# Computing the modulation vectors in four 32-column tiles of the tensor engine, and splitting every weight on VectorE

## The chip, the cores and the metric

One core of a Trainium2 chip runs the whole program. The metric is the device time of one execution in microseconds. The kernel before took 2518.86 us, the median of three executions (2513.32 to 2525.78).

## The reference, cut to what matters

Two stacks of layers run one after the other on one sequence of S = 256 tokens of width D = 1024. The first stack mixes with forgetting attention and with latent attention, each followed by a mixture of 16 experts; every norm in it is modulated by vectors made from a single condition vector `c`. The second stack has four mixers (retention, MoBA, differential attention, retention), each followed by an MLP.

```python
c_act = jax.nn.silu(c)                                     # (1, 1024)
for layer in range(2):
    sh1, sc1, g1, sh2, sc2, g2 = jnp.split(c_act @ w_mod[layer] + b_mod[layer], 6, axis=-1)   # w_mod[layer]: 1024 x 6144
    h = modulate(rmsnorm(x, norm_g), sh1, sc1)             # h * (1 + sc1) + sh1
    x = x + g1[:, None, :] * mixer(h)                      # forgetting attention, then latent attention
    h = modulate(rmsnorm(x, ffn_norm_g[layer]), sh2, sc2)
    x = x + g2[:, None, :] * grouped_moe(h)
    # behind layer 0: two more vectors, c_act @ kv_w_mod + kv_b_mod (1024 x 2048), for the keys and values of layer 1
```

So there are 14 modulation vectors of 1024 elements, each the product of the condition vector with a 1024 x 1024 piece of a matrix: 4 MB of float32 weights are read for every one of them, and used once.

## The kernel before, in words

**Phases.** The first block runs `start`, `fgt` (forgetting attention), `moe0`, `lat_pre` and `lat_heads` (latent attention) and `moe1`; the second block `ret0`, `mlp0`, `moba`, `mlp1`, `diff`, `mlp2`, `ret1` and `mlp3`. By TensorE's first product of each phase these are, in us of the span: 0 to 44, 44 to 232, 232 to 532, 532 to 579, 579 to 704, 704 to 997; then 997 to 1221, 1221 to 1409, 1409 to 1574, 1574 to 1760, 1760 to 1936, 1936 to 2122, 2122 to 2329 and 2329 to 2522.

**Weights.** A piece of weights of 1 MB is loaded by SyncE's queue into one of five buffers `raw` (`load()`). For the dense layers `unit()` then makes two halves of it in pieces of 128x1024: ScalarE casts `wh` (L147), and `wl = raw - wh` (L153) is what the cast left out. Each dense product is three products of these halves (`wh` by the activation's high half, `wh` by its low half, `wl` by its high half; L169 to L171, L180 to L182, L197 to L199). Which engine makes `wl` is set by the table `SPL`: in five phases every `wl` (in `lat_heads` every second one) goes to GpSimd, in all others to VectorE:

```python
SPL = {'fgt': (1, 0), 'latpre': (1, 0), 'latheads': (2, 0), 'moba': (1, 0), 'diff': (1, 0)}
sh = SPL.get(self.ph, ())
eng = nc.gpsimd if sh and self.nu % sh[0] in sh[1:] else nc.vector
```

127 of the 526 splits are GpSimd's. The experts' weights in the two MoE phases aren't split: there float32 products read `raw` and pairs of other buffers, and two experts' streams of 64 columns stand side by side in the array (L1347).

**Modulations.** `prepare()` puts silu(c) into a tile `c` of 128x8 (element k * 128 + p in row p, column k). `mod()` makes one vector in four steps, of which each loads 4 rows of 128 by 512 columns. On VectorE a step multiplies every row piece by its element of `c` and adds it to an accumulator `macc` of 128x512 (L811 for the first of eight, L813 for the rest). After two steps, half of the vector is there in 128 partial sums per column, and `total()` sums them with four small float32 products (`macc` as the stationary operand, a column of ones moving, L824) into four columns of the result.

The 56 steps stand in a list, `self.queue`. `fill()` takes all or some of them, and `spare()`, called between the pieces of the mixers, takes as many as the next entry of a table (`PLAN0`, `PLAN1`) says. A step's four operations are issued in one go, and the `total()` of the vector before behind the first of them. 8 steps run in the start, 24 in forgetting attention, 4 in the first MoE, 5 in `lat_pre` and 15 in `lat_heads`. In the start, the eight steps of the first two vectors are put in another order, so that the first halves of both come first (L1506).

**Order of the work.** A tile scheduler orders each engine's instructions from the order in the program and the buffers (`pat()`, `ppj()` and `psc()` hand out banks of PSUM: for `pat()` two in most phases and six in `lat_pre`). Each engine works its own list off in order.

**The chains spoken of below.** In `moba` and `diff` the scores need normed queries and keys: L648 sums squares of 8 heads, L652 scales them, the inverse root is worked out by tiny integer and float operations on VectorE (L253 to L263, over 128x16 there and 128x1 or 128x2 elsewhere), L657 and L659 multiply, and TensorE transposes the result (L663). The softmax takes maxima as it moves the scores out of PSUM (L531) and turns them into the bias of the exponential (L533, 128x2). In `diff` the output of a head is normed once more (the same root, L259 among it) into `o` (L710), which TensorE transposes (L210). In `lat_pre`, L869 makes the low half `h2l` of an activation that the projections read.

Of the kernel before, what the change touches and what calls it, by code (L numbers as in the profile page):

```python
# [10 lines left out]
F32 = mybir.dt.float32  # L11
# [4 lines left out]
OP = mybir.AluOpType  # L16
# [14 lines left out]
GU = 2  # L31
GE = 4
HOLD = dict(ret0=2, mlp0=2, mlp1=2, mlp2=2, mlp3=2, moba=4)
SPL = {'fgt': (1, 0), 'latpre': (1, 0), 'latheads': (2, 0), 'moba': (1, 0), 'diff': (1, 0)}
HL = 6
WX = 2
HOMES = "rhrhxhrhrhxhr"
# [47 lines left out]
class Net:  # L85
# [51 lines left out]
    def unit(self, ap, k, n):  # L137
# [4 lines left out]
        for k0 in range(0, k, step):  # L142
# [5 lines left out]
            self.nu += 1  # L148
            sh = SPL.get(self.ph, ())
            eng = nc.gpsimd if sh and self.nu % sh[0] in sh[1:] else nc.vector  # L150
# [568 lines left out]
    def prepare(self):  # L719
# [31 lines left out]
        self.ones = self.b1.tile([128, 128], F32, name="ones", tag="ones")  # L751
        nc.vector.memset(self.ones, 1.0)

    def rope(self):

        nc, I = self.nc, self.I
        pi = self.b1.tile([128, NT], I32, name="pi", tag="pi")
        nc.scalar.dma_start(pi, I["positions"].rearrange("b (t p) -> p (b t)", p=128))
        pf = self.b1.tile([128, NT], F32, name="pf", tag="pf")
        nc.vector.tensor_copy(pf, pi)  # L760
        inv = self.b1.tile([128, 16], F32, name="inv", tag="inv")
        nc.scalar.dma_start(inv, bass.AP(tensor=self.C["narrow"].tensor, offset=self.C["narrow"].offset + 768,
                                         ap=[[0, 128], [1, 16]]))
        ang = self.b1.tile([128, NT, 16], F32, name="ang", tag="ang")
        n = self.b1.tile([128, NT, 16], F32, name="angn", tag="angn")
        for t in range(NT):
            nc.vector.tensor_scalar(ang[:, t, :], inv, pf[:, t:t + 1], None, op0=OP.mult)
        big = 12582912.0
        nc.vector.tensor_scalar(n, ang, 1.0 / (2 * math.pi), big, op0=OP.mult, op1=OP.add)
        nc.vector.tensor_scalar(n, n, big, None, op0=OP.subtract)  # L770
        c1 = 6.28125
        c2 = float((np.array([2 * math.pi - c1], np.float32).view(np.uint32) & np.uint32(0xfffff000)).view(np.float32)[0])
        c3 = 2 * math.pi - c1 - c2
        for cc in (c1, c2, c3):
            nc.vector.scalar_tensor_tensor(ang, n, -cc, ang, op0=OP.mult, op1=OP.add)
        s = self.b1.tile([128, NT, 16], F32, name="hs", tag="hs")
        nc.scalar.activation(s, ang, AF.Sin, scale=0.5)
        nc.vector.scalar_tensor_tensor(ang, ang, -1.0, ang, op0=OP.mult, op1=OP.max)
        nc.vector.tensor_scalar(ang, ang, -0.5, math.pi / 2, op0=OP.mult, op1=OP.add)
        nc.scalar.activation(n, ang, AF.Sin)  # L780
        self.rc = self.b1.tile([128, NT, 2, 16], F32, name="rc", tag="rc")
        self.rsn = self.b1.tile([128, NT, 2, 16], F32, name="rsn", tag="rsn")
        for j in range(2):
            nc.vector.scalar_tensor_tensor(self.rsn[:, :, j, :], s, 2.0, n, op0=OP.mult, op1=OP.mult)
            nc.vector.scalar_tensor_tensor(self.rc[:, :, j, :], s, -2.0, s, op0=OP.mult, op1=OP.mult)
        nc.vector.tensor_scalar(self.rc, self.rc, 1.0, None, op0=OP.add)
# [5 lines left out]

    def mod(self, w, c0, bias, gain=None):
        nc = self.nc
        self.nmod += 1
        col = self.b1.tile([128, 8], F32, name="mod", tag="mod%d" % self.nmod)

        spot = {}  # L800

        def step(u):
            half = u // 2
            r = self.load(self.rows(w, u % 2 * 4, 4, c0 + half * 512, 512), 4, 512)
            if u % 2 == 0:
                spot["acc"] = self.mods.tile([128, 512], F32, name="macc", tag="macc")
            acc = spot["acc"]
            for k in range(4):
                kk = u % 2 * 4 + k
                if kk == 0:  # L810
                    i = nc.vector.tensor_scalar(acc, r[:, k, :], self.c[:, 0:1], None, op0=OP.mult)  # L811
                else:
                    i = nc.vector.scalar_tensor_tensor(acc, r[:, k, :], self.c[:, kk:kk + 1], acc, op0=OP.mult,  # L813
                                                       op1=OP.add)
            with self.tc.issue_after(i.ins):
                self.finish()
            if u % 2:
                self.finish = lambda: total(acc, slice(4 * half, 4 * half + 4))

        def total(acc, c):  # L820
            self.finish = lambda: None
            ps = self.pat()
            for f in range(4):
                nc.tensor.matmul(ps[:, f:f + 1], acc[:, f * 128:f * 128 + 128], self.ones[:, 0:1], start=True, stop=True)  # L824
            self.mark = nc.vector.tensor_tensor(col[:, c], ps[:, 0:4], bias[:, c], OP.add).ins
            if gain is not None:
                nc.vector.scalar_tensor_tensor(col[:, c], col[:, c], 1.0, gain[:, c], op0=OP.add, op1=OP.mult)
        self.queue += [lambda u=u: step(u) for u in range(4)]
        return col

# [655 lines left out]
    def first_block(self):  # L1486
        I = self.I
        with self.tc.tile_pool(name="b1", bufs=1) as b1, \
                self.tc.tile_pool(name="mods", bufs=2) as mods:
            self.b1, self.mods = b1, mods  # L1490
            self.queue, self.plan = [], []
            self.finish = lambda: None
            self.nmod = 0
            self.plan = list(PLAN0)

            def layer(i, j, gain=None):

                return self.mod(I["w_mod"][i], j * D, self.column("b_mod", (6 * i + j) * D), gain)

            with self.phase("start"):  # L1500
                self.prepare()
                self.norm_x()
                ffn = [self.column("ffn_norm_g", i * D) for i in range(2)]
                SH = layer(0, 0)
                A = layer(0, 1, self.column("a_norm_g", 0))
                self.queue = [self.queue[i] for i in (0, 1, 4, 5, 2, 3, 6, 7)]  # L1506
                self.fill()
                self.make_bias()
                self.finish()

            def rope():
                with self.tc.issue_after(self.mark):
                    self.rope()

            def router(i):
                self.finish()
                spot.append(self.router(i, A1, SH1))

            G = layer(0, 2)
            SH1 = layer(0, 3)  # L1520
            A1 = layer(0, 4, gain=ffn[0])
            self.queue.append(lambda: router(0))
            spot = []
            self.queue.append(rope)
            G1 = layer(0, 5)
            kSH = self.mod(I["kv_w_mod"], 0, self.column("kv_b_mod", 0))
            kA = self.mod(I["kv_w_mod"], D, self.column("kv_b_mod", D), self.column("kv_norm_g", 0))
            SH2 = layer(1, 0)
            A2 = layer(1, 1, gain=self.column("b_norm_g", 0))
            self.forgetting(A, SH, G)  # L1530
            self.moe(0, A1, SH1, G1, spot[0])
            SH, A = SH2, A2
            self.left = len(self.queue)
            G = layer(1, 2)
            SH1 = layer(1, 3)
            A1 = layer(1, 4, gain=ffn[1])
            self.queue.append(lambda: router(1))
            G1 = layer(1, 5)
            self.plan = list(PLAN1)
            self.latent(kA, kSH, A, SH, G)  # L1540
            self.moe(1, A1, SH1, G1, spot[1])
            self.pending = self.diag
# [47 lines left out]
```

## Time and profile before

| | |
|---|---|
| median of three executions | 2518.86 us |
| the profiled execution | 2524.33 us, of which its span 2522.5 us |
| mean granted clock of TensorE | 0.955 of 2.4 GHz |
| PE busy | 2276.9 us (90%), 13606 instructions |
| VectorE (DVE) busy | 1310.5 us (52%), 2465 instructions |
| ScalarE (ACT) busy | 985.5 us (39%), 1622 instructions |
| GpSimd (POOL) busy | 297.4 us (12%), 139 instructions |
| DMA | 541.96 MB, 215 GB/s over the span |

The busy shares are averages over phases with different limits, so they are read by phase. "PE" is TensorE's products and "PEld" its loads of stationary weights, which overlap with them; DVE, ACT, POOL and SP are VectorE, ScalarE, GpSimd and SyncE. The granted clock is the mean of two levels, 1.2 GHz (0.5) and 2.4 GHz (1.0), in the stretch. L153 is line 153 of the kernel before; the changed kernel's lines stand 5 to 7 further down from `prepare()` on.

### The profile page before, as it was taken

Reading aid. Unit: us, or ns where it says so; the run is one execution under the profiler, and the core shown is the slowest. Engines: PE = TensorE matmul, PEld = TensorE weight load, DVE = VectorE, ACT = ScalarE, POOL = GpSimd, SP = SyncE. Lnnn points to the kernel's source line nnn. Section 1 sums busy time; section 2 is a strip of 40 time slices with the busy share of each in tenths; the row PEclk is TensorE's granted clock in tenths of the full one; section 3 lists DMA queues with packets and bytes.
Section 4 is the critical chain, followed back from the end, with each engine's and each line's share of the span. In section 5 each row is a group of like instructions: output and inputs, shape, how many; then the busy total and the mean of one; then the engine's idle time right before and its main releaser. Section 6 shows DMA issues by size and latency. Waiting matters only on the chain.

```text
span 2522.5 us, 34039 instructions
## 1 busy us (share of the span) xinstructions
PE 2276.9 (90%) x13606; PEld 1779.1 (71%) x13606; DVE 1310.5 (52%) x2465; ACT 985.5 (39%) x1622; POOL 297.4 (12%) x139
## 2 busy tenths in 40 slices
PE   4887999959989997979999888999678999999999
PEld 3787443348854333867899778998677998887997
DVE  7877110087840003645655544655667555665654
ACT  2444111146521112434444445444455444444443
POOL 2443000032200000000000443001441000000000
PEclk9888999979989998989999989999899999999999
DMA  9768999956689995554555423555423555544552
GB/s 302 244 206 290 348 365 395 354 191 206 228 306 400 397 387 212 165 169 150 167 191 191 158 79 117 170 198 169 135 87 125 190 185 182 176 151 155 177 191 84
DMA packets 310470, 541.96 MB, mean 215 GB/s; under 512 B 15752, under 2 KB 158720, under 8 KB 310304
## 3 DMA queue, kind: packets, MB, share of 16 engines
q1 hardware_dynamic: 298288, 528.84, 60.3%
q10 hardware_dynamic: 12016, 10.85, 1.4%
q8 instruction: 111, 1.82, 0.3%
q14 instruction: 55, 0.45, 0.1%
HBM read 538.57 MB, written 4.22 MB: 215 GB/s over the span
## 4 chain that ended last, share of the span: by engine, by line
PE 50%; DVE 7%; ACT 1%; issue 1%; ACTq 1%; DMA 0%
DVE rsa L259 1%; ACTq L588 1%; DVE wl L153 1%; DVE rsy L253 1%; DVE rsy L263 1%; DVE m L533 1%; DVE rsy L254 0%; DVE p L531 0%; PE acc__mlp__16304 L199 0%; PE acc__mlp__19715 L198 0%; PE acc__mlp__9577 L199 0%; PE acc__mlp__16302 L199 0%; PE acc__mlp__9576 L197 0%; PE acc__mlp__9575 L199 0%; PE acc__mlp__19713 L198 0%
## 5 line engine op out<-in xcount | busy, mean ns | idle before, releaser
L147 ACT CAST wh<-raw 128x1024 fp32r<-128x1024 f32 (+4 forms) x526 | 523.8, 1020 | 462.0 <-issue 71.8
L153 DVE TENSOR_TENSOR wl<-raw,wh 128x1024 fp32r<-128x1024 f32 (+1 forms) x399 | 476.4, 1215 | 380.7 <-ACT wh L147 378.0
L153 POOL TENSOR_TENSOR wl<-raw,wh 128x1024 fp32r<-128x1024 f32 (+4 forms) x127 | 287.3, 2280 | 1577.9 <-ACT wh L147 1570.3
L813 DVE SCALAR_TENSOR_TENSOR macc<-raw,c,macc 128x512 f32<-128x512 f32 x196 | 190.6, 973 | 5.6 <-DMA raw<-in_w_mod_dram 2.4
L535 ACT ACTIVATE p<-p,m 128x128 f32<-128x128 f32 (+1 forms) x128 | 57.0, 448 | 36.5 <-DVE m L533 36.3
L398 ACT CAST aTh<-rl 128x512 fp32r<-128x512 f32 x56 | 34.7, 620 | 78.4 <-DVE rl L396 78.4
L399 DVE TENSOR_TENSOR aTl<-rl,aTh 128x512 fp32r<-128x512 f32 x56 | 38.8, 693 | 38.5 <-ACT aTh L398 38.5
L276 ACT ACTIVATE junk<-x 128x512 f32<-128x512 f32 x52 | 32.7, 629 | 64.5 <-DVE x L341 33.3
L259 DVE SCALAR_TENSOR_TENSOR rsa<-rsy,rsh 128x1 f32<-128x1 f32 x186 | 50.4, 302 | 3.1
L396 DVE TENSOR_TENSOR rl<-rl 128x512 f32<-128x512 f32 x56 | 38.3, 685 | 0.0
L218 ACT CAST hTh<-xg 128x512 fp32r<-128x512 f32 (+1 forms) x36 | 21.2, 604 | 27.5 <-DVE xg L215 24.8
L219 DVE TENSOR_TENSOR hTl<-xg,hTh 128x512 fp32r<-128x512 f32 (+1 forms) x36 | 27.3, 777 | 2.4 <-ACT hTh L218 2.2
L533 DVE TENSOR_SCALAR m<-m 128x2 f32<-128x2 f32 x64 | 26.7, 418 | 0.5
L263 DVE SCALAR_TENSOR_TENSOR rsy<-rsa,rsy 128x2 f32<-128x2 f32 (+2 forms) x141 | 24.9, 177 | 3.9
L648 DVE TENSOR_REDUCE qss<-sq 128x8 f32<-128x512 f32 x16 | 10.9, 684 | 29.1 <-ACT sq L647 29.1
L535 ACT ACTIVATION_READ_ACCUMULATOR p<-p,m 128x1 f32 x128 | 24.1, 189 | 0.0
L1384 PE MATMUL acc__moe__2320<-dv,back 64*128 64x512 f32 x32 | 18.0, 641 | 2.7 <-ACT dv L1375 2.7
L1384 PE MATMUL acc__moe__6093<-dv,back 64*128 64x512 f32 x32 | 18.0, 641 | 2.5 <-ACT dv L1375 2.5
L1384 PE MATMUL acc__moe__2321<-dv,back 64*128 64x512 f32 x32 | 18.0, 641 | 0.0
L1384 PE MATMUL acc__moe__6094<-dv,back 64*128 64x512 f32 x32 | 18.0, 641 | 0.0
L824 PE MATMUL at__latpre__4036<-ones,macc 128*128 128x1 f32 x8 | 1.8, 351 | 16.6 <-DVEq L1231 16.6
L1384 PE MATMUL acc__moe__2323<-dv,back 64*128 64x512 f32 x32 | 16.8, 605 | 0.0
(3889 smaller groups left out, 7365.2 us busy)
## 6 DMA issues: line engine op xcount, KB each, us to landing
raw<-in_w_up_dram SPq DMA_DIRECT2D x64, 1024.0 KB, 5.5
raw<-in_w_down_dram SPq DMA_DIRECT2D x64, 1024.0 KB, 5.5
raw<-in_w_mod_dram SPq DMA_DIRECT2D x48, 1024.0 KB, 5.2
raw<-in_ret_w_in_dram SPq DMA_DIRECT2D x48, 1024.0 KB, 5.2
raw<-in_exp_w_gate_dram SPq DMA_DIRECT2D x40, 1024.0 KB, 12.4
raw<-in_exp_w_down_dram SPq DMA_DIRECT2D x34, 1024.0 KB, 13.0
raw<-in_exp_w_up_dram SPq DMA_DIRECT2D x30, 1024.0 KB, 11.3
wh<-in_exp_w_up_dram SPq DMA_DIRECT2D x34, 512.0 KB, 8.7
```

Source lines behind the costliest of these rows:

```text
L147: nc.scalar.copy(h[:, :m * n], p)
L153: eng.tensor_tensor(l[:, :m * n], p, h[:, :m * n].bitcast(F32), OP.subtract)
L259: nc.vector.scalar_tensor_tensor(a[:, c], y[:, c], h[:, c], y[:, c], op0=OP.mult, op1=OP.mult)
L263: nc.vector.scalar_tensor_tensor(y, a, 1.5, y, op0=OP.add, op1=OP.mult)
L276: nc.scalar.activation(junk[:, :w], p, AF.Square, scale=n ** -0.5, accum_out=ss[:, i, j:j + 1])
L396: nc.vector.tensor_tensor(rl, rl, rl, OP.mult)
L398: nc.scalar.copy(h, rl)
L399: nc.vector.tensor_tensor(aT[1][:, 2 * j:2 * j + 2, :].rearrange("p k t -> p (k t)"), rl, h.bitcast(F32), OP.subtract)
L533: nc.vector.tensor_scalar(mx, mx, -1.0, None, op0=OP.mult)
L535: nc.scalar.activation(p[:, m, :], p[:, m, :], AF.Exp, bias=mx[:, m:m + 1], accum_out=rs[:, m, s:s + 1])
L813: i = nc.vector.scalar_tensor_tensor(acc, r[:, k, :], self.c[:, kk:kk + 1], acc, op0=OP.mult, op1=OP.add)
L1384: mm(acc[tok][half], back[c, e % 4, tok * 128:tok * 128 + 128], dv[c, :], start=e == 0, stop=e == 15)
```

## The change

The modulations' long sums move to TensorE. A step loads 2 rows of 128 by all 1024 columns of its vector, still 1 MB, and makes four float32 products of one bank: the stationary operand is one column of `c`, repeated 32 times, the moving operand 512 columns of one row, and the result 32 partitions of the bank, a tile of 32 columns of the array for each of the four. VectorE then copies the bank into `macc` (first step) or adds it (the three others). Behind the fourth step every row of the four groups of 32 holds a sum: groups 0 and 2 of the first 512 columns, 1 and 3 of the last. `total()` now comes once per vector and adds two rows by products with a small table `pick`, that has a one in rows 0 and 64 (first column) and 32 and 96 (second): eight products instead of twice four. The steps of the start run in their plain order.

With `SPL` empty, every `wl` is made on VectorE.

```diff
-SPL = {'fgt': (1, 0), 'latpre': (1, 0), 'latheads': (2, 0), 'moba': (1, 0), 'diff': (1, 0)}
+SPL = {}
...
+        self.pick = self.b1.tile([128, 2], F32, name="pick", tag="pick")
+        nc.vector.memset(self.pick, 0.0)
+        for j in range(4):
+            nc.vector.memset(self.pick[32 * j:32 * j + 1, j % 2:j % 2 + 1], 1.0)
...
         def step(u):
-            half = u // 2
-            r = self.load(self.rows(w, u % 2 * 4, 4, c0 + half * 512, 512), 4, 512)
-            if u % 2 == 0:
+            r = self.load(self.rows(w, 2 * u, 2, c0, 1024), 2, 1024)
+            ps = self.pat()
+            for k in range(2):
+                for half in range(2):
+                    j = 32 * (2 * k + half)
+                    nc.tensor.matmul(ps[j:j + 32, :], self.c[:, 2 * u + k:2 * u + k + 1].to_broadcast([128, 32]),
+                                     r[:, k, half * 512:half * 512 + 512], start=True, stop=True)
+            if u == 0:
                 spot["acc"] = self.mods.tile([128, 512], F32, name="macc", tag="macc")
-            acc = spot["acc"]
-            for k in range(4):
-                kk = u % 2 * 4 + k
-                if kk == 0:
-                    i = nc.vector.tensor_scalar(acc, r[:, k, :], self.c[:, 0:1], None, op0=OP.mult)
-                else:
-                    i = nc.vector.scalar_tensor_tensor(acc, r[:, k, :], self.c[:, kk:kk + 1], acc, op0=OP.mult,
-                                                       op1=OP.add)
+                i = nc.vector.tensor_copy(spot["acc"], ps)
+            else:
+                i = nc.vector.tensor_tensor(spot["acc"], ps, spot["acc"], OP.add)
             with self.tc.issue_after(i.ins):
                 self.finish()
-            if u % 2:
-                self.finish = lambda: total(acc, slice(4 * half, 4 * half + 4))
+            if u == 3:
+                self.finish = lambda: total(spot["acc"])
...
-        def total(acc, c):
+        def total(acc):
...
-            for f in range(4):
-                nc.tensor.matmul(ps[:, f:f + 1], acc[:, f * 128:f * 128 + 128], self.ones[:, 0:1], start=True, stop=True)
-            self.mark = nc.vector.tensor_tensor(col[:, c], ps[:, 0:4], bias[:, c], OP.add).ins
+            for f in range(8):
+                nc.tensor.matmul(ps[:, f:f + 1], acc[:, f % 4 * 128:f % 4 * 128 + 128], self.pick[:, f // 4:f // 4 + 1],
+                                 start=True, stop=True)
+            self.mark = nc.vector.tensor_tensor(col, ps[:, 0:8], bias, OP.add).ins
...
-                self.queue = [self.queue[i] for i in (0, 1, 4, 5, 2, 3, 6, 7)]
                 self.fill()
```

The change moves instructions on two engines at places that the prediction speaks of. The first is VectorE in `moba`, around the sums of squares of the second group of heads (L648) and the first links of the inverse root (to L263). Before:

```order
L648 TENSOR_REDUCE qss<-sq 128x8
L564 TENSOR_TENSOR o<-at__moba__11565,rs 128x256
L219 TENSOR_TENSOR aTl<-at__moba__11575,aTh 128x2x128
L648 TENSOR_REDUCE qss<-sq 128x8
L652 TENSOR_SCALAR qss<-qss 128x16
L253 TENSOR_SCALAR rsy<-qss 128x16
L255 TENSOR_SCALAR rsh<-qss 128x16
L254 TENSOR_SCALAR rsy<-rsy 128x16
L261 TENSOR_TENSOR rsa<-rsy 128x16
L262 TENSOR_TENSOR rsa<-rsa,rsh 128x16
L263 SCALAR_TENSOR_TENSOR rsy<-rsa,rsy 128x16
```

Now:

```order
L153 TENSOR_TENSOR wl<-raw,wh 128x1024
L219 TENSOR_TENSOR aTl<-at__moba__11646,aTh 128x2x128
L153 TENSOR_TENSOR wl<-raw,wh 128x1024 x2
L648 TENSOR_REDUCE qss<-sq 128x8
L652 TENSOR_SCALAR qss<-qss 128x16
L253 TENSOR_SCALAR rsy<-qss 128x16
L255 TENSOR_SCALAR rsh<-qss 128x16
L254 TENSOR_SCALAR rsy<-rsy 128x16
L261 TENSOR_TENSOR rsa<-rsy 128x16
L153 TENSOR_TENSOR wl<-raw,wh 128x1024
L262 TENSOR_TENSOR rsa<-rsa,rsh 128x16
L263 SCALAR_TENSOR_TENSOR rsy<-rsa,rsy 128x16
```

Four splits now stand here, three ahead of the second sum of squares and one between two links of the root; before they were in the list of GpSimd.

The second place is TensorE in `fgt`, from the end of the decay's products to the score products of the second group (`sc` are banks of scores, `pj` of projections, `at` those that `pat()` hands out). Before:

```order
L972 MATMUL at__fgt__925<-ncum,both 128x256 x2
L523 MATMUL sc__fgt__959<-kT,qT 128x128
L523 MATMUL sc__fgt__999<-kT,qT 128x256
L523 MATMUL sc__fgt__1000<-kT,qT 128x256
L824 MATMUL at__fgt__944<-ones,macc 128x1 x4
L523 MATMUL sc__fgt__999<-kT,qT 128x256
L523 MATMUL sc__fgt__1000<-kT,qT 128x256
L180 MATMUL pj__fgt__1062<-hTh,wh 128x256
```

Now:

```order
L979 MATMUL at__fgt__946<-ncum,both 128x256 x2
L979 MATMUL at__fgt__952<-ncum,both 128x256 x2
L523 MATMUL sc__fgt__1024<-kT,qT 128x256
L523 MATMUL sc__fgt__1025<-kT,qT 128x256
L523 MATMUL sc__fgt__1024<-kT,qT 128x256
L814 MATMUL at__fgt__960<-raw,c 32x512 x4
L814 MATMUL at__fgt__968<-raw,c 32x512 x4
L523 MATMUL sc__fgt__1025<-kT,qT 128x256
L814 MATMUL at__fgt__976<-raw,c 32x512 x4
L545 MATMUL at__fgt__1005<-ident,p 128x128
```

Where one total of four small products stood, three steps of four 32-column products (L814) stand between and behind the score products.

## Rows read from the trace of the kernel before

**Rows 1.** The page, costliest groups (busy us, mean ns, idle before, releaser)
```profile
L153 DVE TENSOR_TENSOR wl<-raw,wh 128x1024 fp32r<-128x1024 f32 (+1 forms) x399 | 476.4, 1215 | 380.7 <-ACT wh L147 378.0
...
L813 DVE SCALAR_TENSOR_TENSOR macc<-raw,c,macc 128x512 f32<-128x512 f32 x196 | 190.6, 973 | 5.6 <-DMA raw<-in_w_mod_dram 2.4
...
L824 PE MATMUL at__latpre__4036<-ones,macc 128*128 128x1 f32 x8 | 1.8, 351 | 16.6 <-DVEq L1231 16.6
```

**Rows 2.** Busy time by stage: stretch, its length, busy us (instructions) by engine
```profile
core 0: us, PE busy (x) PEld busy (x) DVE busy (x) ACT busy (x) POOL busy (x), PEclk, DMA share, GB/s
0.00:44.00 44.00, 9.53 (x36) 7.60 (x36) 27.42 (x59) 6.37 (x12) 3.99 (x6) 1.00 0.92 311
44.00:232.00 188.00, 161.34 (x1168) 151.87 (x1168) 152.59 (x280) 82.83 (x172) 80.44 (x33) 0.89 0.70 234
232.00:532.00 300.00, 268.01 (x1327) 110.60 (x1325) 62.69 (x144) 51.49 (x95) 11.94 (x8) 0.94 0.94 352
532.00:579.00 47.00, 36.20 (x212) 32.58 (x213) 43.50 (x81) 26.91 (x54) 17.97 (x8) 0.86 0.61 205
579.00:704.00 125.00, 115.77 (x753) 105.67 (x752) 97.02 (x257) 69.81 (x164) 24.94 (x13) 0.93 0.67 225
1409.00:1574.00 165.00, 136.67 (x1017) 127.92 (x1016) 85.39 (x212) 83.02 (x171) 70.85 (x32) 0.93 0.36 115
1760.00:1936.00 176.00, 131.31 (x947) 123.56 (x946) 120.11 (x369) 84.11 (x201) 71.22 (x32) 0.89 0.34 109
```

**Rows 3.** Busy time of line L813 alone in forgetting attention
```profile
core 0: us, DVE busy (x), PEclk, DMA share, GB/s
44.00:232.00 188.00, 96.94 (x84) 0.89 0.70 234
```

**Rows 4.** Busy time of line L153 alone, on VectorE and on GpSimd
```profile
core 0: us, DVE busy (x) POOL busy (x), PEclk, DMA share, GB/s
1409.00:1574.00 165.00, 2.52 (x2) 70.85 (x32) 0.93 0.36 115
1760.00:1936.00 176.00, 2.44 (x2) 71.22 (x32) 0.89 0.34 109
```

**Rows 5.** Groups of instructions on VectorE in moba, 1409 to 1574 us
```profile
L533 DVE TENSOR_SCALAR m<-m 128x2 f32<-128x2 f32 x16 | 11.1, 691 | 0.3
...
L253 DVE TENSOR_SCALAR rsy<-qss 128x16 int32<-128x16 int32 x4 | 8.1, 2033 | 0.1
...
L652 DVE TENSOR_SCALAR qss<-qss 128x16 f32<-128x16 f32 x4 | 5.0, 1239 | 0.1
```

**Rows 6.** The same view in retention, 997 to 1221 us
```profile
L259 DVE SCALAR_TENSOR_TENSOR rsa<-rsy,rsh 128x1 f32<-128x1 f32 x30 | 6.3, 219 | 0.9
...
L253 DVE TENSOR_SCALAR rsy<-oss 128x1 int32<-128x1 int32 x8 | 1.2, 153 | 0.3
```

**Rows 7.** The same view in diff, 1760 to 1936 us
```profile
L259 DVE SCALAR_TENSOR_TENSOR rsa<-rsy,rsh 128x1 f32<-128x1 f32 x54 | 21.2, 433 | 0.9
...
L533 DVE TENSOR_SCALAR m<-m 128x2 f32<-128x2 f32 x16 | 8.6, 538 | 0.1
```

**Rows 8.** Timeline of VectorE and GpSimd in diff (start us, duration us, instruction)
```profile
1778.93 11.76 POOL L153 TENSOR_TENSOR wl<-raw,wh 128x1024 fp32r<-128x1024 f32 x5 [5.45 <-ACT wh L147]
...
1783.77 2.32 DVE L253 TENSOR_SCALAR rsy<-qss 128x16 int32<-128x16 int32 x1
1786.01 2.42 DVE L255 TENSOR_SCALAR rsh<-qss 128x16 f32<-128x16 f32 x1
1788.35 2.38 DVE L254 TENSOR_SCALAR rsy<-rsy 128x16 int32<-128x16 int32 x1
```

**Rows 9.** TensorE's waits: waiting line <- releaser: us, times, longest us
```profile
PE pj__latpre__4322 L171 <- DVE h2l L869: 10.1, 2, 7.9
...
PE at__diff__15921 L210 <- DVE o L710: 7.0, 1, 7.0
PE at__moba__11419 L663 <- DVE qk L659: 6.9, 1, 6.9
```

**Rows 10.** Timeline of TensorE in the first MoE (start us, duration us, instruction)
```profile
293.81 0.59 PE L1347 MATMUL pj__moe__2476<-wl,xgt 128*64 128x512 f32 x1
293.82 0.59 PE L1347 MATMUL pj__moe__2476<-raw,xgt 128*64 128x512 f32 x1
294.24 0.59 PE L1347 MATMUL pj__moe__2476<-wl,xgt 128*64 128x512 f32 x1
...
294.77 0.66 PE L1360 MATMUL at__moe__2491<-ident,gu 128*128 128x128 f32 x4
```

More of the change, by code (lines that the diff above doesn't have):

```diff
@@ L826, in total @@
             if gain is not None:
-                nc.vector.scalar_tensor_tensor(col[:, c], col[:, c], 1.0, gain[:, c], op0=OP.add, op1=OP.mult)
+                nc.vector.scalar_tensor_tensor(col, col, 1.0, gain, op0=OP.add, op1=OP.mult)
         self.queue += [lambda u=u: step(u) for u in range(4)]
```

## The prediction

> **What bounds the kernel now.** Read first the busy times stage by stage [rows 2]; a stage is a phase of the program, and its bounds are where TensorE's first product of that phase starts. Two kinds of stage matter. In the mixers of the first block (44 to 232 and 579 to 704 us) TensorE is busy 161 of 188 and 116 of 125 us, VectorE 153 and 97, and the granted clock is 0.89 and 0.93, that is 1.2 GHz instead of 2.4 for 22% and 14% of the time. In the two attention layers of the second block (1409 to 1574 and 1760 to 1936 us) TensorE is busy 137 of 165 and 131 of 176 us: there something else makes it wait. The table of waits says what: the transposes wait up to 6.9 us for qk (L659) in moba and up to 7.0 us for o (L710) in diff, both ends of a chain of tiny VectorE operations [rows 9].
>
> Why that chain is slow is read from the operations themselves. In retention, where GpSimd does nothing, L253 takes 153 ns; in moba, where GpSimd splits weights, the same line takes 2033 ns, L652 1239 and L533 691 [rows 5, 6]. The timeline shows the moment: a run of five splits on GpSimd from 1778.93 to 1790.69 us, 2.35 us each, and inside it one L253 of 16 columns that takes 2.32 us [rows 8]. It waits for the GpSimd instruction to end. L255 and L254 behind it do the same.
>
> **The change, part by part.** 56 steps of modulations leave VectorE (8 in the start, 24 in forgetting attention, 4 in the first MoE, 5 in latpre, 15 in latheads). Each was one L811 and seven L813 per two steps and is now four products on TensorE and one copy or add of 512 columns on VectorE. 127 splits leave GpSimd for VectorE.
>
> *One step on TensorE.* No row shows four column tiles. The nearest shows two, of 64 columns: two matmul records start together (293.81 and 293.82) and the next two 0.43 us later [rows 10]. A float32 product is two such records, so two tiles take 0.86 us. Four at once would also take 0.86, in twos 1.71, one after another 3.42. Leaving the 64-column tiles for a whole-array product costs 0.10 more (294.24 to 294.77, 0.53 instead of 0.43), and each step changes twice: about 1.05 us at full clock is an estimate from these rows, with 3.6 as the other end. I take 1.05, because the two-tile row shows that a second tile costs nothing.
>
> *One step on VectorE.* It loses four operations at 0.97 us on average [rows 1] (1.15 in forgetting, 96.94 us for 84 [rows 3], since GpSimd stands in their way too) and gains one of about 0.7. One split there takes 1.22 us [rows 1] against 2.2 on GpSimd (70.85 us for 32 [rows 4]).
>
> *Start, 0.* Its DMA share is 0.92 [rows 2]: eight units of 1 MB have to land whoever uses them. Bounds: -3 (the last four VectorE operations) and +4 (eight small products in the total instead of four; four take 1.8 us [rows 1]).
>
> *Forgetting, +2.* VectorE falls from 153 by about 105 (L813 and L811), and rises by 24 x 0.7 and 33 x 1.2: some 105 are left, so TensorE is the bound. It gets 24 x 1.05 = 25 us. Floor: all of the 27 idle us filled and the slow clock (22% of 188 us at half speed, some 17 us of busy time) gone, 161 + 25 - 17 = 169, which is -19. Ceiling: nothing filled, +25. In order's listing the new products stand between the score products, where TensorE waits anyway, so I take a value a little under the middle.
>
> *First MoE, +1.* Four steps are 4 us on a TensorE that is busy 268 of 300 us; the VectorE work that held up the branch at its end (TensorE waits 16.6 us there [rows 1]) shrinks. Bounds -4 and +4.
>
> *latpre, -5.* TensorE waits 10.1 us for h2l, which stands behind macc on VectorE [rows 9]; that goes, and 5 x 1.05 comes. Bounds -10 and +3.
>
> *latheads, +6.* TensorE is busy 116 of 125 us; 15 steps are 16 us. Floor: the idle 9 and the half-clock loss of some 8 come back, -1. Ceiling +16.
>
> *moba, -15.* Three lines alone lose to GpSimd: L533 16 x (691 - 153), L253 4 x (2033 - 153), L652 4 x (1239 - 153) = 8.6 + 7.5 + 4.3 = 20 us, all on the chain to qk or p; L254 and L255 are of the same kind and in the same chain, so some 25. In their place come 32 x 1.22 = 39 us of splits, but only where they stand in that chain do they delay it: in the changed order about two of a group's eight do (L153 between L261 and L262, and one among the maxima), 8 x 1.22 = 10. Net -15. Bounds: -28, TensorE's whole idle time, and +10.
>
> *diff, -14.* L259 54 x (433 - 219) = 11.6 and L533 16 x (538 - 153) = 6.2 [rows 6, 7], and the run L253, L255, L254 took some 7 us once instead of 0.5 [rows 8]: 25 to 30 on the chain. More of the splits (32 x 1.22 = 39) stand between its links, about a third, 13. Net -14. Bounds -28 and +12.
>
> The stages after 1936 us have no GpSimd splits and no modulations, nor has the second MoE: 0. Where the VectorE stall goes, TensorE is late next in the first block, and the same chain, without locks, in the second.
>
> **Sum:** 0 + 2 + 1 - 5 + 6 - 15 - 14 = -25 us. The profiled execution took 2524.33 us, 5.5 above the median of 2518.86; set against the median, 2494 us.
>
> A rule speaks against the change. The Trainium skill, "SBUF — State Buffer", section "A bandwidth-pool intuition that's wrong (but worth ruling out)", gives TensorE's reading of the moving operand as about 614 GB/s. By it one step, which streams 128 x 512 float32 values through four tiles twice, 2.1 MB, would take 3.4 us. The trace does not agree: two tiles stream 0.52 MB in 0.43 us [rows 10], 1.2 TB/s. But a limit at twice the page's figure would not show in any row here; that is the next rival.
>
> **Rivals.**
> - *Tiles in twos* (0.15). If TensorE cannot stream more than the two 512-column operands that the rows show at a time, a step takes 0.86 us more. In the 48 steps behind the start that is +41, nearly all on a TensorE that is already the bound there: +16, 2535 us, slower. It decides against the change from a step of some 1.6 us. For it: no row shows four. Against: the second tile is free.
> - *One after another* (0.05). Four streams of 0.86 us, 2.57 more per step, 48 times: +123, about 2617 us. Against it stand the two tiles that do overlap.
> - *The splits take the place of the locks* (0.15). If VectorE's in-order queue delays the chains by as much as GpSimd did, moba and diff gain nothing: +4, 2523 us, no change. For it: 39 us of splits come for 20 to 30 of locks, and in diff a split stands between most links. Against: beside TensorE's projections they cost nothing.
> - *The first block gains too* (0.13). With VectorE half empty the gaps close and the clock stays up: forgetting -15, latheads -1 instead of +2 and +6, so -49, 2470 us. Against: TensorE gets 46 us there and has 36 idle.
>
> **How the numbers follow.** The forecast has 0.52. A measurement of this kernel can tell about 0.5%, 12.6 us, from no change. Faster than 2506: the forecast save 0.02, and the fourth rival, 0.63. Slower than 2531: most of the first rival and the second, 0.19. Between: the third and the edges, 0.18. The range from 2455 to 2540 takes in the fourth rival with the floors of moba and diff, and the first rival; it leaves out the second and the worst of the first.
>
> **What would show it.** Right: L814's records four at a time, 0.43 us from one set of four to the next; L253, L652 and L533 near 150 ns everywhere; TensorE busy over 90% in moba, and its waits for qk and o halved; forgetting attention about as long as before with a clock above 0.93. Wrong: records of L814 that start two by two or one by one; PE's waits for qk as long as before behind L153 on VectorE; or a forgetting stage that is 15 us longer or shorter.

## The result, and the profile after

The changed kernel takes 2458.34 us, the median of four executions (2453.07 to 2466.2), against 2521.63 of the kernel before (four executions too): 63 us less, where 25 were forecast. The ratio, taken of the means, is 0.9756 (95% interval 0.9717 to 0.9794). Its profiled execution took 2453.07 us, so between the two profiles lie 71 us. (The one before stands a little above its median, this one a little below.)

Where the time went is seen by stage, each from TensorE's first product of the phase to that of the next, in us (rounded after subtracting):

| stage | before | after | difference | forecast |
|---|---|---|---|---|
| start | 44.0 | 41.4 | -2.6 | 0 |
| forgetting attention | 188.0 | 179.7 | -8.3 | +2 |
| first MoE | 300.5 | 301.7 | +1.2 | +1 |
| lat_pre | 46.8 | 45.9 | -1.0 | -5 |
| lat_heads | 124.4 | 131.5 | +7.1 | +6 |
| moba | 165.1 | 140.9 | -24.2 | -15 |
| diff | 175.7 | 134.0 | -41.6 | -14 |

The other seven stages came out 1.8 us shorter in all. So the five stages of the first block in the table gave 3.6 us, and two stages of the second block, in which there isn't one modulation, gave 66.

The first view is the busy time by stage of the changed kernel (stretch, its length, busy us and instructions of each engine, granted clock, DMA share, GB/s), to be set beside [rows 2]:

```profile
core 0: us, PE busy (x) PEld busy (x) DVE busy (x) ACT busy (x) POOL busy (x), PEclk, DMA share, GB/s
0.00:41.00 41.00, 21.48 (x99) 7.91 (x100) 9.69 (x36) 5.42 (x11) 0.20 (x4) 1.00 0.90 320
41.00:221.00 180.00, 175.80 (x1353) 145.01 (x1352) 94.74 (x234) 84.05 (x173) 0.00 (x0) 0.96 0.71 245
...
569.00:700.00 131.00, 130.25 (x864) 107.19 (x864) 70.70 (x219) 67.14 (x158) 0.00 (x0) 0.95 0.62 215
1404.00:1545.00 141.00, 129.80 (x1018) 119.75 (x1017) 86.98 (x244) 82.34 (x171) 0.00 (x0) 1.00 0.40 128
1731.00:1865.00 134.00, 123.64 (x945) 114.14 (x944) 108.97 (x401) 81.64 (x199) 0.00 (x0) 0.97 0.45 144
```

In forgetting attention and `lat_heads` TensorE is now busy for 176 of 180 and 130 of 131 us: there it is the bound, and next to nothing is left to fill. In `moba` and `diff` its idle time fell from 28 to 11 and from 45 to 10 us, and for the same products it was busy 7 to 8 us less, with a granted clock of 1.00 instead of 0.93 and of 0.97 instead of 0.89.

Of VectorE's 87.0 and 109.0 us in these two stages, the splits alone are (the same view, line L153 alone):

```profile
core 0: us, DVE busy (x), PEclk, DMA share, GB/s
...
1404.00:1545.00 141.00, 37.87 (x34) 1.00 0.40 128
1731.00:1865.00 134.00, 38.48 (x34) 0.97 0.45 144
```

All other instructions of VectorE are the same as before, 210 in `moba` and 367 in `diff`. Added over their own lengths they took 91.5 and 135.7 us before, and take 60.1 and 95.7 now: 31.5 and 40.0 us less. They take the same 60.1 and 95.7 us in the run with the splits alone, below. So this is time for which GpSimd's splits held them up. (The records of neighbouring instructions overlap a little, so these sums are more than VectorE's busy time.) VectorE's groups in `moba`, beside [rows 5], show the small operations at lengths of 160 to 175 ns:

```profile
L533 DVE TENSOR_SCALAR m<-m 128x2 f32<-128x2 f32 x16 | 2.6, 161 | 0.2
...
L253 DVE TENSOR_SCALAR rsy<-qss 128x16 int32<-128x16 int32 x4 | 0.7, 175 | 0.1
L652 DVE TENSOR_SCALAR qss<-qss 128x16 f32<-128x16 f32 x4 | 0.7, 173 | 0.1
```

Two more lines, L219 and L254, lost some 4 us each. Before:

```profile
L219 DVE TENSOR_TENSOR hTl<-xg,hTh 128x512 fp32r<-128x512 f32 x4 | 6.4, 1629 | 0.1
...
L254 DVE TENSOR_SCALAR rsy<-rsy 128x16 int32<-128x16 int32 (+1 forms) x5 | 5.2, 1037 | 0.0
```

Now:

```profile
L219 DVE TENSOR_TENSOR hTl<-xg,hTh 128x512 fp32r<-128x512 f32 x4 | 2.6, 684 | 0.0
...
L254 DVE TENSOR_SCALAR rsy<-rsy 128x16 int32<-128x16 int32 (+1 forms) x5 | 0.9, 174 | 0.0
```

In `diff` L259 takes 215 ns instead of 433 [rows 7]:

```profile
L259 DVE SCALAR_TENSOR_TENSOR rsa<-rsy,rsh 128x1 f32<-128x1 f32 x54 | 9.3, 215 | 0.4
```

The new step on TensorE, first by its tile (count, then min/median/max of one record in ns, and the first and last start), then in the timeline:

```profile
L814 PE MATMUL at__fgt__858<-raw,c x8: 592/604/616, 99.6 to 100.1; 128*32 128x512 f32 x8
```

```profile
99.63 1.06 PE L814 MATMUL at__fgt__858<-raw,c 128*32 128x512 f32 x8
100.62 0.39 PE L169 MATMUL pj__fgt__875<-wh,hTh 128*128 128x256 f32 x1
```

Eight records of 0.6 us each start within 0.5 us. They start in two sets of four, the second 0.45 us behind the first, so four run at a time, and the next product starts 0.99 us behind the first. The estimate was 1.05.

The Trainium skill ("SBUF — State Buffer", "A bandwidth-pool intuition that's wrong (but worth ruling out)") gives 614 GB/s for TensorE's moving operand in bf16; the prediction left the type out. Taken as a limit for these float32 operands, by which a step would take 3.4 us, the figure does not hold here: the four tiles stream 2.1 MB in 0.99 us, 2.1 TB/s.

### The profile page after: what moved, and what is told of

It is laid out like the page before. It is cut to its first block, busy times and chain, and to the rows that moved or that the text cites. A ratio compares the mean times of both kernels' runs of the same rounds, so it can differ in the third digit from the quotient of the medians.

```text
span 2451.3 us, 34695 instructions
## 1 busy us (share of the span) xinstructions
PE 2315.3 (94%) x14054; PEld 1758.8 (72%) x14054; DVE 1180.6 (48%) x2410; ACT 982.1 (40%) x1622; POOL 10.1 (0%) x12
## 4 chain that ended last, share of the span: by engine, by line
PE 51%; DVE 5%; ACT 1%; ACTq 1%; issue 1%; DMA 0%; DVEq 0%
DVE wl L153 2%; ACTq L588 1%; ACT wh L147 1%; DVE rsa L259 0%; DVE rsy L263 0%; PE acc__mlp__19785 L199 0%; PE acc__mlp__16374 L197 0%; PE acc__mlp__12926 L197 0%; PE acc__mlp__9647 L197 0%; PE acc__mlp__19783 L199 0%; PE acc__mlp__9648 L197 0%; PE acc__mlp__16375 L197 0%; PE acc__mlp__12926 L198 0%; PE acc__mlp__12927 L197 0%; PE acc__mlp__19784 L197 0%
## 5 line engine op out<-in xcount | busy, mean ns | idle before, releaser
L153 DVE TENSOR_TENSOR wl<-raw,wh 128x1024 fp32r<-128x1024 f32 (+4 forms) x526 | 614.2, 1187 | 413.6 <-ACT wh L147 408.9
L259 DVE SCALAR_TENSOR_TENSOR rsa<-rsy,rsh 128x1 f32<-128x1 f32 x186 | 34.4, 215 | 2.7
L219 DVE TENSOR_TENSOR hTl<-xg,hTh 128x512 fp32r<-128x512 f32 (+1 forms) x36 | 23.5, 671 | 2.0 <-ACT hTh L218 1.8
L263 DVE SCALAR_TENSOR_TENSOR rsy<-rsa,rsy 128x2 f32<-128x2 f32 (+2 forms) x141 | 22.6, 160 | 3.4
L535 ACT ACTIVATION_READ_ACCUMULATOR p<-p,m 128x1 f32 x128 | 24.2, 189 | 0.0
L1391 PE MATMUL acc__moe__2359<-dv,back 64*128 64x512 f32 x32 | 18.1, 645 | 4.4 <-ACT dv L1382 4.4
L1391 PE MATMUL acc__moe__6164<-dv,back 64*128 64x512 f32 x32 | 18.0, 641 | 2.7 <-ACT dv L1382 2.7
L1391 PE MATMUL acc__moe__6165<-dv,back 64*128 64x512 f32 x32 | 18.0, 641 | 0.0
L1391 PE MATMUL acc__moe__2360<-dv,back 64*128 64x512 f32 x32 | 18.0, 641 | 0.0
L1391 PE MATMUL acc__moe__2361<-dv,back 64*128 64x512 f32 x32 | 17.2, 618 | 0.0
L1391 PE MATMUL acc__moe__2362<-dv,back 64*128 64x512 f32 x32 | 16.8, 605 | 0.0
L1391 PE MATMUL acc__moe__6166<-dv,back 64*128 64x512 f32 x32 | 16.8, 605 | 0.0
L1391 PE MATMUL acc__moe__6167<-dv,back 64*128 64x512 f32 x32 | 16.8, 605 | 0.0
```

The costliest lines, as they stand in the source:

```text
L153: eng.tensor_tensor(l[:, :m * n], p, h[:, :m * n].bitcast(F32), OP.subtract)
L219: nc.vector.tensor_tensor(lo[:, k0:k0 + n, tok * 128:tok * 128 + 128], pv, d.bitcast(F32), OP.subtract)
L259: nc.vector.scalar_tensor_tensor(a[:, c], y[:, c], h[:, c], y[:, c], op0=OP.mult, op1=OP.mult)
L263: nc.vector.scalar_tensor_tensor(y, a, 1.5, y, op0=OP.add, op1=OP.mult)
L535: nc.scalar.activation(p[:, m, :], p[:, m, :], AF.Exp, bias=mx[:, m:m + 1], accum_out=rs[:, m, s:s + 1])
L1391: mm(acc[tok][half], back[c, e % 4, tok * 128:tok * 128 + 128], dv[c, :], start=e == 0, stop=e == 15)
```

## Experiments

The change has two halves that touch different places. Two theories stood against each other: that the gain is the end of GpSimd's blocking of VectorE, and that it comes from the modulations (or from low halves that are ready earlier). All ratios are to the kernel before, whose median in these runs was 2520.6 to 2520.8 us.

**1. The modulations alone** (`mods_only`): the changed kernel with the old table of splits.

```diff
-SPL = {}
+SPL = {'fgt': (1, 0), 'latpre': (1, 0), 'latheads': (2, 0), 'moba': (1, 0), 'diff': (1, 0)}
```

> The change without its other half: modulations on TensorE, the 127 splits back on GpSimd. Theory of the blocked VectorE (GpSimd's splits hold up VectorE's small operations, and that is nearly all of the gain in the second block): moba is 165 us again instead of 141 and diff 176 instead of 134, so about 2458 + 66 = 2524 us, with the first block within 10 us of that of the changed kernel. Rival, the gain hangs on the modulations (less VectorE work, buffers free earlier): moba and diff stay within 10 us of 141 and 134, and the time under 2480.

Measured: 2548.19 us, 1.0107 (1.0076 to 1.0138): slower than before. `moba` took 166.6 and `diff` 171.7 us, as the first theory says. The first block took 27 us more than in the changed kernel instead of at most 10 (forgetting attention 192.2, `lat_pre` 54.4, `lat_heads` 135.4 us), so GpSimd's splits cost time there too, even with L813 gone. The busy times of forgetting attention and `moba` in this run:

```profile
core 0: us, PE busy (x) PEld busy (x) DVE busy (x) ACT busy (x) POOL busy (x), PEclk, DMA share, GB/s
42.00:234.00 192.00, 181.53 (x1352) 150.93 (x1353) 70.15 (x199) 83.56 (x173) 73.90 (x33) 0.93 0.66 228
...
1431.00:1597.00 166.00, 138.72 (x1015) 130.04 (x1014) 84.81 (x212) 82.77 (x171) 70.57 (x32) 0.92 0.36 115
```

**2. The splits alone** (`splits_only`): the kernel before with the empty table.

```diff
-SPL = {'fgt': (1, 0), 'latpre': (1, 0), 'latheads': (2, 0), 'moba': (1, 0), 'diff': (1, 0)}
+SPL = {}
```

> The other half alone: modulations on VectorE as before, every split on VectorE. Theory of the blocked VectorE: moba 141 and diff 134 us, so some 2522 - 66 = 2456 us; in forgetting attention L813 falls from 1154 ns to some 750, which frees 34 us of VectorE, and 40 us of splits come, so that stage stays within 8 us of its 188. Rival, the modulations on TensorE are needed to make room for the splits in the first block: forgetting attention takes over 196 us and the time is 2465 or more.

Measured: 2422.06 us, 0.9607 (0.958 to 0.9634), and so 36 us faster than the whole change. `moba` 140.7 and `diff` 134.2 us, as expected. Forgetting attention came out at 160.3 us, not within 8 of 188, and `lat_heads` at 116.4:

```profile
core 0: us, PE busy (x) PEld busy (x) DVE busy (x) ACT busy (x) POOL busy (x), PEclk, DMA share, GB/s
44.00:204.00 160.00, 149.30 (x1167) 141.67 (x1168) 137.07 (x312) 82.79 (x172) 0.00 (x0) 0.96 0.82 276
...
545.00:662.00 117.00, 112.15 (x752) 103.47 (x751) 95.12 (x271) 69.06 (x164) 0.00 (x0) 0.96 0.68 232
```

```profile
core 0: us, DVE busy (x), PEclk, DMA share, GB/s
44.00:204.00 160.00, 61.59 (x84) 0.96 0.82 276
```

The second fence is L813 alone: 733 ns each, against 1154 before [rows 3], with the modulations still on VectorE. VectorE does carry both jobs, 137 of 160 us.

The two runs and the two kernels make a square, in us: neither half 2520.6 (2521.6 in the changed kernel's own comparison), modulations alone 2548.2, splits alone 2422.1, both 2458.3. The splits are worth -98.6 by themselves and -89.9 beside the modulations, and the modulations cost +27.6 beside GpSimd's splits and +36.3 without them. By stage, from splits alone to both, the modulations' price is -2.3 in the start, +19.4 in forgetting attention (24 steps), +3.6 in the first MoE (4), +2.6 in `lat_pre` (5) and +15.1 in `lat_heads` (15). In forgetting attention the steps take 26.4 us of TensorE (L814, shown with the next run). TensorE's busy time there grew by just that, from 149.3 to 175.8 us, and only 6.5 us of it came out of its idle time, which fell from 10.7 to 4.2.

**3. Two column tiles instead of four** (`twos`): the price of a step's time on TensorE, changed kernel otherwise.

```diff
-                    j = 32 * (2 * k + half)
+                    j = 32 * half
...
-                                     r[:, k, half * 512:half * 512 + 512], start=True, stop=True)
+                                     r[:, k, half * 512:half * 512 + 512], start=k == 0, stop=k == 1)
```

VectorE's copies and adds and the total take 64 rows accordingly.

> The changed kernel with each step's four products in two column tiles of 32 instead of four, two products one after the other in each, everything else alike. If four tiles really run side by side, a step takes 0.86 us longer: 39 of the 48 steps behind the start lie in forgetting attention and the latent heads, where TensorE is busy 98 and 99% of the time, so +34 to +41 us, 2492 to 2499 us. If four tiles run two by two anyway, 2458 us, no change.

Measured: 2493.27 us, 0.9893 (0.9867 to 0.992), 34.9 more than the changed kernel. L814 alone in forgetting attention, in the changed kernel and then in this one:

```profile
core 0: us, PE busy (x) PEld busy (x), PEclk, DMA share, GB/s
41.00:221.00 180.00, 26.40 (x192) 4.42 (x192) 0.96 0.71 245
```

```profile
core 0: us, PE busy (x) PEld busy (x), PEclk, DMA share, GB/s
40.00:239.00 199.00, 50.01 (x192) 10.22 (x192) 0.96 0.67 229
```

24 steps go from 1.10 to 2.08 us each, 23.6 in all, and the stage grows by 18.7, from 179.7 to 198.4; in `lat_heads` L814 goes from 14.9 to 27.7 us, 12.8 more, and the stage grows by 17.4, from 131.5 to 149.0. Together the two stages grow by 36.1 us for 36.4 more of L814, though neither stage does so by itself; in `lat_heads` the granted clock was also lower, 0.93 instead of 0.95. Four tiles do run side by side, and on a TensorE with few gaps most of what a step takes is paid for. That is how the modulations come to cost 36 us in the square.

**4. The blocking without late halves** (`spare_splits`): every `wl` on VectorE, and the old 127 subtractions once more on GpSimd into a tile that nobody reads.

```diff
+IDLE = {'fgt': (1, 0), 'latpre': (1, 0), 'latheads': (2, 0), 'moba': (1, 0), 'diff': (1, 0)}
...
+            sh = IDLE.get(self.ph, ())
+            if sh and self.nu % sh[0] in sh[1:]:
+                spare = self.sp.tile([128, self.part], F32R, name="spare", tag="spare")
+                nc.gpsimd.tensor_tensor(spare[:, :m * n], p, h[:, :m * n].bitcast(F32), OP.subtract)
```

> The changed kernel, with VectorE making every wl, and beside it the same 127 subtractions once more on GpSimd into a tile that nobody reads. Theory of the blocked VectorE: the blocking alone comes back, so moba and diff take 155 to 176 us each again and the time is 2500 to 2530 us. Rival, late halves (GpSimd's 2.2 us against 1.2 made TensorE wait for wl): nothing waits for the spare results, so moba and diff stay within 6 us of 141 and 134 and the time under 2475.

Measured: 2626.46 us, 1.0422 (1.0381 to 1.0463), with `moba` 201.9 and `diff` 197.1 us: worse than forecast and worse than before. Nobody waits for the spare tile, so late halves of GpSimd's aren't needed for the loss. That GpSimd holds buffers longer is not ruled out by the run alone, but TensorE's waits speak against it: the longest are for qk (13.4 us in `moba`, 12.6 in `diff`) and o (9.8), and those for a `wl`, now VectorE's, come to 7.5 us in `moba` and to none in `diff`. Nor does TensorE wait for a `wl` of GpSimd's in `moba` or `diff` before, where its 28 and 45 us of waits are for qk, p, o, activations and their halves. What I hadn't thought of is that VectorE's splits are blocked themselves (groups of VectorE in `moba`, and the two stages' busy times; lines stand a few further down here, L261 is L255 and L155 is L153):

```profile
L155 DVE TENSOR_TENSOR wl<-raw,wh 128x1024 fp32r<-128x1024 f32 (+1 forms) x34 | 66.4, 1978 | 4.4 <-ACT wh L149 4.4
L261 DVE TENSOR_SCALAR rsh<-qss 128x16 f32<-128x16 f32 x4 | 9.3, 2331 | 0.0
```

```profile
1451.00:1652.00 201.00, 144.25 (x1013) 134.28 (x1011) 140.84 (x244) 83.59 (x173) 85.14 (x32) 0.85 0.29 91
1839.00:2036.00 197.00, 137.42 (x945) 127.59 (x944) 166.14 (x401) 83.81 (x201) 85.94 (x32) 0.85 0.31 100
```

VectorE's time grew by 54 and 57 us, and the stages by 61 and 63.

**5. One input instead of two** (`spare_copies`): as in 4, with a copy on GpSimd.

```diff
-                nc.gpsimd.tensor_tensor(spare[:, :m * n], p, h[:, :m * n].bitcast(F32), OP.subtract)
+                nc.gpsimd.tensor_copy(spare[:, :m * n], p)
```

> As the run with spare subtractions, but with GpSimd's instruction a copy of raw, with one input instead of two. If any GpSimd instruction over 128x1024 that overlaps VectorE blocks it for its whole length, moba and diff come out as with the spare subtractions (202 and 197 us); if it takes an instruction that reads two operands, VectorE's small operations stay near 160 ns and both stages within 6 us of 141 and 134.

Measured: 2480.83 us, 0.9842 (0.982 to 0.9865), `moba` 148.7 and `diff` 147.7 us, between the two forecasts. A copy does block. In VectorE's timeline of `diff`, with two copies running on GpSimd from 1755.28 to 1759.46, L259 and L260 (L253 and L254 of the changed kernel) take 1.03 and 1.01 us each, and L261, which falls between, 0.16:

```profile
1755.28 4.18 POOL L159 CAST spare<-raw 128x1024 fp32r<-128x1024 f32 x2 [7.35 <-DMA raw<-in_diff_w_in_dram]
```

```profile
1756.32 1.03 DVE L259 TENSOR_SCALAR rsy<-var 128x2 int32<-128x2 int32 x1
1757.26 0.16 DVE L261 TENSOR_SCALAR rsh<-var 128x2 f32<-128x2 f32 x1
1757.33 1.21 DVE L155 TENSOR_TENSOR wl<-raw,wh 128x1024 fp32r<-128x1024 f32 x1
1758.47 1.01 DVE L260 TENSOR_SCALAR rsy<-rsy 128x2 int32<-128x2 int32 x1
```

But 24 of the 32 copies fall into each stage, the others ahead of it, and GpSimd is busy with them for 29 to 31 us, not 85; the loss is smaller with it.

**6. Shorter instructions on GpSimd** (`short_splits`): the kernel before, each of GpSimd's splits in pieces of 256 columns.

```diff
-                eng.tensor_tensor(l[:, :m * n], p, h[:, :m * n].bitcast(F32), OP.subtract)
+                cut = 256 if eng is nc.gpsimd else m * n
+                for s in range(0, m * n, cut):
+                    e = min(s + cut, m * n)
+                    eng.tensor_tensor(l[:, s:e], p[:, s:e], h[:, s:e].bitcast(F32), OP.subtract)
```

> The kernel before, with each of GpSimd's splits cut into four instructions of 256 columns. Theory of the blocked VectorE: a blocked operation waits for the end of the one GpSimd instruction in its way, so L253 in moba falls from 2033 to some 600 to 800 ns and L533 from 691 to some 300; moba then takes 145 to 155 us instead of 165 and diff 145 to 160 instead of 176, unless GpSimd's own time grows so far that TensorE waits for wl. Rival, VectorE waits until GpSimd's list is empty: nothing changes in L253, and both stages stay at 165 and 176.

Measured: 2484.29 us, 0.9856 (0.9834 to 0.9879). In `moba` L253 (here L256) falls from 2033 to 660 ns, beside pieces of 774 ns: the wait ends with one instruction of GpSimd, not when its list is empty.

```profile
L256 DVE TENSOR_SCALAR rsy<-qss 128x16 int32<-128x16 int32 x4 | 2.6, 660 | 0.1
```

```profile
L156 POOL TENSOR_TENSOR wl<-raw,wh 128x256 fp32r<-128x256 f32 x119 | 86.7, 774 | 69.0 <-ACT wh L147 69.0
```

The stages fell less than forecast: 161.1 and 164.6 us; forgetting attention fell to 167.0. GpSimd is now busy for 87 us in `moba` instead of 71, TensorE still waits 21 us for qk there, and VectorE's total is 83.0 us where it was 85.4. L253 and L533 lost less, but other links of the same chain lost more: L261 (here L264) took 175 ns beside whole splits and takes 494 beside pieces, L262 went from 174 to 490 and L263 from 172 to 395.

```profile
L264 DVE TENSOR_TENSOR rsa<-rsy 128x16 f32<-128x16 f32 x12 | 5.9, 494 | 0.4
```

So pieces in a row meet one link of a chain after the other, each for less than one piece.

**7. More splits on VectorE** (`spare_on_vector`): the changed kernel with spare subtractions on VectorE, 32 in `moba` and 16 in `diff`.

```diff
+IDLE = {'moba': (1, 0), 'diff': (2, 0)}
...
+                nc.vector.tensor_tensor(spare[:, :m * n], p, h[:, :m * n].bitcast(F32), OP.subtract)
```

> The changed kernel with spare subtractions on VectorE behind its own splits: 32 more in moba (39 us) and 16 more in diff (20 us). If splits delay the chains as the prediction charged them (about 10 us for 32 in moba, about 6 for 16 in diff), the stages take 151 and 140 us. If they lie beside TensorE's projections, 141 to 144 and 134 to 137, although VectorE in diff is then busy for 129 of 134 us.

Measured: 2462.06 us, 0.9768 (0.9746 to 0.979), `moba` 145.0 and `diff` 140.4 us: +4.1 for 32 splits, 0.13 us each, and +6.4 for 16, 0.40 each. The prediction had charged 10 for 32 (0.31) and 13 for 32 (0.41). In `moba` most of a split is hidden, in `diff` the charge was right. (These splits come on top of the change's own; what its own cost was not run by itself.)

**8. TensorE where it has nothing else to do** (`start_tensor`): all splits on VectorE, and of the modulations only the start's eight steps on TensorE.

```diff
+TM = 2
...
+        if self.nmod > TM:
+            return self.mod_dve(w, c0, bias, gain, col)
```

`mod_dve` has the step and the total of the kernel before.

> Every split on VectorE, and on TensorE only the eight modulation steps of the start, where TensorE has nothing else to do; the other 48 on VectorE. The start took 41.4 us in the changed kernel against 43.7 with the splits alone moved, so about 2 us less than that run's 2422: 2418 to 2422 us. If the steps in the later stages cost what the runs show (36 us for all 56), this beats both kernels; if the order of the queue matters more, it comes out over 2425.

Measured: 2421.77 us, 0.9611 (0.9593 to 0.9629): the same as with the splits alone. The start took 40.9 instead of 43.7 us, but forgetting attention 164.9 instead of 160.3, with a granted clock of 0.93 there instead of 0.96. Why the clock was lower, and whether that comes with the edit, wasn't tried. Both versions beat the change by 36 us.

## Why the prediction was right and wrong

**Faster, and from the end of the blocking: right.** The signs that were named came: L253, L652 and L533 at 160 to 175 ns, TensorE busy for 130 of 141 us in `moba` (92%), and a forgetting stage less than 15 us off with a clock of 0.96. Of the waits for qk and o, up to 7.0 us each before [rows 9], the longest left in TensorE's table of waits (us in total, times, longest) is this:

```profile
PE at__diff__16060 L210 <- DVE o L710: 2.6, 1, 2.6
```

**The step on TensorE: right.** 1.05 us was taken, 0.99 to 1.10 measured. (That a further tile is free was argued from a row with two tiles and none with one; `twos` shows it from two to four.) The first rival (tiles in twos) is refuted by the records of L814, and its price, +41 for 0.86 us more per step, was close: +34.9 for 0.98 in `twos`. The same records refute the second, one tile after another.

**First block: near in sum, within its bounds in each stage** (+4 forecast, -3.6 measured). In part that was luck. In forgetting attention the splits by themselves brought -27.7 and the modulations on top of them +19.4, in `lat_heads` -8.0 and +15.1; two large terms cancel. The prediction had priced 25 us of steps there, but had no term for what the end of GpSimd's blocking gives there, only idle time and a slow clock that might go.

**`moba` -15 and `diff` -14: the step that failed.** -24 and -42 were measured, 37 of the 46 us by which the sum missed between the two profiles. The mechanism was right, but one term was too small, one was put at nothing, and one was too large in one stage:

- *The blocked time on VectorE, above all in `diff`.* The prediction added up a few lines, 25 us in `moba` and 25 to 30 in `diff`; over all lines it was 31.5 and 40.0. In `moba` the five lines that it named lost 26.7, as it said, and L219 and L279, which it didn't name, 4.8. In `diff` L259 and L533 lost 17.8, as it said. But L253, L254 and L255 lost 13.0, where one run of them was counted with 6.5, and L263, L624, L693 and L706, unnamed, lost 8.7. Three of these lines in `diff` before:

```profile
L693 DVE SCALAR_TENSOR_TENSOR p<-p,rs 128x128 f32<-128x128 f32 (+1 forms) x16 | 8.3, 547 | 0.0
L254 DVE TENSOR_SCALAR rsy<-rsy 128x2 int32<-128x2 int32 (+1 forms) x13 | 6.6, 506 | 0.0
...
L706 DVE TENSOR_SCALAR dss<-dss 128x2 f32<-128x2 f32 x8 | 3.4, 429 | 13.8 <-ACT junk L704 13.8
```

and now:

```profile
L693 DVE SCALAR_TENSOR_TENSOR p<-p,rs 128x128 f32<-128x128 f32 (+1 forms) x16 | 6.3, 412 | 0.0
...
L254 DVE TENSOR_SCALAR rsy<-rsy 128x2 int32<-128x2 int32 (+1 forms) x13 | 2.1, 164 | 0.0
...
L706 DVE TENSOR_SCALAR dss<-dss 128x2 f32<-128x2 f32 x8 | 1.3, 164 | 2.9 <-ACT junk L704 2.7
```

- *The clock was counted in the first block and put at nothing in the second*, though [rows 2] show 0.93 and 0.89 for `moba` and `diff`. TensorE was busy 6.9 and 7.7 us less at 1.00 and 0.97.
- *The splits' charge* was right for `diff` and, by the spare splits, some 6 us too high for `moba`.

What is left of the two stages is TensorE's idle time, which fell by 17 and 34 us. In `moba` that is near the 15 forecast, and most of the miss there is the clock. In `diff` it is 20 more than forecast, and the blocked time was some 13 more. The terms don't add up to either stage: 31.5 less 4 for splits is more than the 17 in `moba`, and 40.0 less 13 is less than the 34 in `diff`. Which of the blocked operations TensorE waited for was not shown. The floor that the prediction set for `diff`, -28, was wrong by its own row: TensorE's idle time was 176 - 131 = 45 us.

**The rivals.** *The splits take the place of the locks* is refuted by both stages. *The first block gains too* gave 2470, near the 2458 that came, but for a reason that didn't hold: the first block as a whole gained 3.6 us, where this rival asked for 20. What no rival named is the shape of the answer: one half of the change worth 90 to 99 us, and the other a loss of 28 to 36 that it hides.

## What to carry to other kernels

When a change has two halves, price each by itself, and run each by itself: here the half that was described first costs 36 us, and without it the other would have been a 3.9% gain instead of 2.4%. Work that moves to TensorE is free only where TensorE has gaps: in a stage in which it was busy 149 of 160 us, 26 us of new products made the stage 19 us longer. And before GpSimd is given work "beside" VectorE, compare VectorE's small operations in a stage with GpSimd at work and in one without: add up what they differ by over all lines, not the longest few. What a stage gives back still has to be run: here it was 24 us for a sum of 31.5, and 42 for 40.0.

## What the runs showed of the hardware

- While a GpSimd instruction over SBUF runs, a VectorE operation with its operands in SBUF may wait for that one instruction to end: such an operation took 2.3 us beside a split of 128x1024, 0.66 beside pieces of 128x256 and 1.0 beside a copy, instead of 0.17. The Trainium skill ("SBUF — State Buffer", "SBUF: two separate sides") states it as an exclusive lock on a shared pair of ports, held for the whole instruction by whichever engine starts first. The runs agree, in the other direction too: with VectorE splitting as well, GpSimd's own subtraction takes 85.14 / 32 = 2.66 us instead of 70.85 / 32 = 2.21.
- A copy on GpSimd, with one input, blocks too, and splits of VectorE's (two inputs) are blocked as its small operations are: 1.98 us instead of 1.16 in `moba`.
- Cutting GpSimd's instruction in four shortens the longest waits (L253 from 2.03 to 0.66 us) and yet leaves VectorE's time in `moba` nearly as it was, 83.0 us instead of 85.4, since more operations wait.
- Four 32-column tiles of float32 products run side by side: 8 records in 0.99 us, with a change of tile size behind them. The same products in two tiles take 2.08 us a step instead of 1.10.
